# A bias-table tile 32 bytes longer: every later SBUF tile moves from 32 past a multiple of 64 bytes to a multiple of 64

## Chip, cores and metric

The kernel runs on one core of a Trainium2 chip. The metric is the device time of one execution in microseconds. Three runs of the kernel before took 2123.62, 2129.89 and 2130.25 us, median 2129.89 us.

## What is computed

A decoder trunk of two layers over 256 tokens of 2048 channels, batch 1, all in float32:

```python
cond = silu(c)
for i in range(2):
    sh1, sc1, g1, sh2, sc2, g2 = split(cond @ w_ada[i] + b_ada[i], 6)
    h = rmsnorm(x, norm_g[i, 0]) * (1 + sc1) + sh1
    y = pool_mixer(h) if i == 0 else moba_attention(h, w_qkv, w_o, rel_table)
    x = x + g1 * y
    h = rmsnorm(x, norm_g[i, 1]) * (1 + sc2) + sh2
    u = causal_conv3(h @ w_up[i]) + conv_b[i]        # 2048 -> 2 * 5632
    x = x + g2 * ((silu(u_gate) * u_val) @ w_down[i])
return rmsnorm(x, final_g)
```

The pool mixer takes trailing-window means and one 512 x 512 product per group; the attention is one causal block of 256 tokens with a T5 relative-position bias, whose 32 x 16 table `rel_table` is the table of this change.

## The kernel before

Activations lie with channels on the 128 partitions and the 256 tokens along the row. Every large product (`w_up`, `w_down`, `w_qkv`, `w_o`) is made as three float32r matmuls in place of one float32 matmul: weights and activations are each split into a rounded part `hi` and a rest, and `hi*hi`, `hi*rest` and `rest*hi` are summed in PSUM (`group_T`, function `products`):

```python
pe.matmul(o, hi[:, kk, w], h[:, 0:S], ...)     # stationary 128 x 128, moving 128 x 256
pe.matmul(o, hi[:, kk, w], h[:, S:S2], ...)
pe.matmul(o, lo[:, kk, w], h[:, 0:S], ...)
```

So in nearly all products a 128 x 128 block of weights (`hi` or `lo`) is the stationary operand, loaded before its matmul, and 256 tokens of an activation tile are the moving operand. Which activation tile that is differs by product: the normed input `h` for `uv` and `ug` (value and gate half of `w_up`) and for `k` and `q`; the tile `act` for `d` (`w_down`); the tile `o` for `wo` (`w_o`). The value projection `v` is turned round (`v_group`): `h` is stationary, and 512 columns of `hi` or `lo` are moving.

Weights arrive in pieces of 1 MiB (`w_load`, queue of SP) in five buffers `raw`; for each half of a piece ScalarE writes `hi` by a copy, VectorE writes `lo` by a subtraction (`w_use`), and three halves later (LAG) TensorE makes the 24 matmuls of that half (`run_half`). Beside this stream run the sums of the conditioning on VectorE (`acc`, `accs`), and convolutions, gates, norms and attention as tasks between halves.

SBUF is laid out by pools. `const` (one buffer for each tile) comes first, then `wp` (`raw`, `hi`, `lo`), then `work` (`act`, `o`, `acc` and the rest). Within a pool a tile begins where the one before ends, rounded up to 32 bytes. The last two tiles of `const` are made in `bias_rows`:

```python
st = const.tile([P, BUCKETS + 1], F32, name="starts")    # 132 bytes a partition, takes 160
rel = const.tile([BUCKETS, H], F32, name="rel")          # 16 floats, 64 bytes
```

`starts` begins at a multiple of 64, so `rel` and all that follows begin 32 bytes past one. Places in bytes of a partition, from the built programs:

```
tile                           before    mod 64   after     mod 64
xT (const)                     18240     0        18240     0
h, pool_room (const)           36864     0        36864     0
starts (const)                 72448     0        72448     0
rel (const)                    72608     32       72608     32
raw, 5 buffers (wp)            72672..   32       72704..   0
hi, 5 buffers (wp)             113632..  32       113664..  0
lo, 5 buffers (wp)             134112..  32       134144..  0
act, o, x, home (work)         156640..  32       156672..  0
acc (work)                     189664    32       189696    0
```

Rows within `hi`, `lo`, `h`, `act` and `o` are cut at multiples of 512 bytes, so a matmul's operand begins at the same place mod 64 as its tile. Before, `h` is thus the one large operand of the products at a multiple of 64; `hi`, `lo`, `act` and `o` are not.

Every operation of PE, DVE and ACT is recorded by a helper and has line 50 in the profile (L50); groups are told apart by the names of their tiles.

Of the kernel before, what the change touches and what calls it, by code (L numbers as in the profile page):

```python
# [9 lines left out]
F32 = mybir.dt.float32  # L10
# [8 lines left out]
EPS = 1e-6  # L19
# [6 lines left out]
def bucket_starts():  # L26
    """First distance of each T5 bucket (the buckets are intervals of distances)."""
    exact = BUCKETS // 2

    def bucket(n):  # L30
        if n < exact:
            return n
        big = exact + int(math.log(n / exact) / math.log(MAX_DIST / exact) * (BUCKETS - exact) + 1e-9)
        return min(big, BUCKETS - 1)

    of = [bucket(n) for n in range(4 * MAX_DIST)]
    return [next((n for n, b in enumerate(of) if b >= want), 1 << 20) for want in range(BUCKETS)]


class InOrder:  # L40
    """An engine whose instructions keep the order they are written in, once `on` is set."""

# [14 lines left out]
def trunk(ctx: ExitStack, tc: tile.TileContext, x, c, norm_g, w_ada, b_ada, pool_w, pool_scale, w_qkv, w_o,  # L57
# [35 lines left out]

# [1 line left out]
    ident = const.tile([P, P], F32, name="ident")  # L95
# [13 lines left out]

# [1 line left out]
    def rows_of(ap1):  # L111
        return ap1.rearrange("(k p) -> k p", p=P)

    def load_rows(name, rows, parts, eng):
        """The tiles of up to 128 rows each; parts: (first row, count, source)."""
        tiles = []
        for done in range(0, rows, P):
            n = min(P, rows - done)
            r = wt([P, P], "vec", 4, f"{name}_r{done}")
            for lo, cnt, src in parts:  # L120
                a, b = max(lo, done), min(lo + cnt, done + n)
                if a < b:
                    eng.dma_start(r[a - done:b - done, :], src[a - lo:b - lo, :])
            tiles.append((done, n, r))
        return tiles
# [8 lines left out]

# [1 line left out]
    c_rows = load_rows("cT", KD, [(0, KD, rows_of(c[0]))], nc.sync)  # L136
# [16 lines left out]
    def transposed(j, name):  # L153
        """Two channel blocks of the input tiles."""
        ps = aux(name)
        for jj in range(2):
            for t in range(NT):
                pe.transpose(ps[:, jj * S + t * P:jj * S + (t + 1) * P],
                                    xn[t][:, (j + jj) * P:(j + jj + 1) * P], ident)
        return ps  # L160
# [15 lines left out]

# [1 line left out]
    mod = const.tile([P, L, 6, KD], F32, name="mod")  # L178
# [4 lines left out]
    def mod_done(l, ch, j0, n, sums):  # L183
        """Columns j0..j0+n of a chunk from their sums."""
        js = slice(j0, j0 + n)
# [23 lines left out]
    def ada_add(l, ch, k, r):  # L209
        """One contraction block on the vector engine: acc += cond[k] * rows."""  # L210
        if (l, ch) not in ada:
            ada[l, ch] = wt([P, D], "acc", 1, f"acc{l}_{ch}")
            ve.tensor_scalar(ada[l, ch], r, cond[:, k:k + 1], None, op0=ALU.mult)
        else:
            a = ada[l, ch]
            ve.scalar_tensor_tensor(a, r, cond[:, k:k + 1], a, op0=ALU.mult, op1=ALU.add)

    def ada_side(l, ch, k):
        """Beside the main stream; the sum over partitions by squares of 32, then over the four quadrants."""
        def use(r):  # L220
# [21 lines left out]
    def slice_load(ch, s, q, pair):  # L242
        """Part of the contraction for 512 columns of a chunk of layer 0, or of two chunks side by side."""
        nk, w = (2, 2) if pair else (4, 1)
# [10 lines left out]
    def slice_use(ch, s, q, pair):  # L255
        """Some blocks of the contraction by TensorE as a row, the others by VectorE."""
        on_pe = PE_BLOCKS[ch if ch < 3 else 3 if s == 0 else 4]
# [45 lines left out]

# [1 line left out]
    sq = {}  # L305
# [23 lines left out]
    def rstd_tokens(m):  # L329
        """1/sqrt(m + EPS) with tokens on partitions, [128, NT]; a Newton step on the table's root."""  # L330
        s = wt([P, NT], "st", 8, "st_s")
# [13 lines left out]
    def root_ready():  # L345
        """Brings the root's table in before the norm needs it."""
        d = wt([P, 1], "st", 8, "st_d")
        ac.activation(d, mean_c, AF.Sqrt)
# [9 lines left out]
    def split(dst, j0, n, src):  # L358
        """An exact sum of two float32r parts: dst[.., :S] the rounded value, dst[.., S:] the rest."""
        hi = dst[:, j0:j0 + n, 0:S]  # L360
        ac.activation(hi, src, AF.Copy)
        ve.tensor_tensor(dst[:, j0:j0 + n, S:S2], src, hi.bitcast(F32), op=ALU.subtract)
# [6 lines left out]
    def scaled(dst, src, l, i, j, vec):  # L369
        """src * g * (1 + scale) + shift of one channel block."""  # L370
        a, b = gsc[:, l, i, j:j + 1], mod[:, l, 3 * i, j:j + 1]
# [5 lines left out]
    def h_block(l, i, j):  # L377
        """One channel block of x * rstd * g * (1 + scale) + shift, in two parts."""
        sh = mod[:, l, 3 * i, j:j + 1]
# [24 lines left out]

# [1 line left out]
    steps = []  # L406
# [20 lines left out]
    def run_tasks(n=1, upto=-1):  # L427
        """The next n tasks, and all up to the last that reads the banks of a group up to `upto`."""
        while tasks and (n > 0 or any(g <= upto for g, _ in tasks)):
            tasks.pop(0)[1]()  # L430
            n -= 1
# [6 lines left out]
    def group_T(src, nk, c0, rhs, done, name, home=None, each=None):  # L438
        """512 columns of src against the transposed activations; done(part) with part(f) the four sums.

        With a home in SBUF the sum is built there, a piece of the stream at a time.
        """
        box = {}
# [58 lines left out]

# [1 line left out]
    acts = {}  # L504
# [6 lines left out]
    def conv_task(o, part, group, f, l, j, then=None):  # L511
        """The causal depthwise convolution and its bias of one channel block."""
        def go():
# [10 lines left out]
    def residual(part, f, g, j):  # L524
        """x += gate * sum."""
        ve.scalar_tensor_tensor(xT[:, j, :], part(f), g[:, j:j + 1], xT[:, j, :], op0=ALU.mult, op1=ALU.add)

    def updated(part, g, og, f):
        """The last of a residual's sums, of two blocks: x and its squares."""
        j = og * 4 + f  # L530
# [131 lines left out]

# [1 line left out]
    bias_dram = dram.tile([H, S + P], F32, name="bias_dram")  # L664

    def bias_rows():
        """e[h, 127 + n] = rel_table[bucket(n), h], and NEG for negative n: rows of every Toeplitz bias."""
        starts = bucket_starts() + [1 << 20]
        st = const.tile([P, BUCKETS + 1], F32, name="starts")
        for b, v in enumerate(starts):  # L670
            nc.gpsimd.memset(st[:, b:b + 1], float(v))
        rel = const.tile([BUCKETS, H], F32, name="rel")
        nc.gpsimd.dma_start(rel, rel_table)
# [20 lines left out]
    def bias_tile(hg):  # L694
        """[p, h, m] = e[h, p + m]; a query p of block t meets key s at m = 255 - s + 128 * (t - 1)."""
        b = wt([P, 4, S], "t4", T4, f"bias{hg}")
# [43 lines left out]
    def scores(hg, t):  # L740
# [7 lines left out]
        for h0 in range(0, 4, per):  # L748
# [4 lines left out]
            bb = b[:, h0:h0 + per, 0:S]  # L753
            # key s reads m = 255 - s for the last block of queries, 127 - s for the first
            br = bb[:, :, n - 1::-1]
# [19 lines left out]
    def heads_out(hg, h0):  # L775
        """Two heads: transposed probabilities times values, split for the output projection."""
        v = att["v", hg]
# [48 lines left out]

# [1 line left out]
    PAD = 16  # L828
# [29 lines left out]
    def pool_sums(g):  # L858
        """Sums over the trailing window, by doubling."""
        w, cur = WINDOWS[g], pool["h"]  # L860
# [12 lines left out]
    def pool_less(g):  # L873
        """The window's mean minus the token."""
        d = pool_d(g)
# [5 lines left out]
    def pool_product(g, f):  # L881
        """One block of columns of the group's matrix."""
        d, w = pool_d(g), pool["w"][g]
# [5 lines left out]
    def pool_out(g):  # L889
        """x += gate * layer_scale * y."""  # L890
        for f in range(GB):
# [3 lines left out]

# [1 line left out]
    fin = {}  # L897

    def final_scaled(og, f, n):
        """x * final_g of n channel blocks."""  # L900
        if f == 0:
# [10 lines left out]
    def final_block(og):  # L912
        """Four channel blocks, tokens back on partitions."""
        if og == 0:
# [30 lines left out]

# [1 line left out]
    ends = []  # L947
# [184 lines left out]
```

## Time and profile before

| | us |
|---|---|
| runs | 2123.62, 2129.89, 2130.25 (median 2129.89) |
| profiled execution, span of its instructions | 2127.2 |
| PE busy in it | 2075.7 (98%) |
| DVE busy | 1643.2 (77%) |
| ACT busy | 958.5 (45%) |
| PE's share of the chain that ended last | 95% |

The profile gives the span of the execution it shows; a device time of its own is not listed beside the three runs, among which the span lies. Matmuls overlap in the records (each is shown for some 280 ns, and the next begins some 120 ns later), so what a matmul costs is read from the distance between starts: the length of an unbroken stretch of one product in the chain of waits, divided by its matmuls.

### The profile page before, as it was taken

How to read it: one execution, taken by the hardware profiler on the slowest of the kernel's cores; microseconds unless marked ns; L12 is line 12 of the kernel's file. 1: busy time of each engine (PE TensorE's matmuls, PEld its weight loads, DVE VectorE, ACT ScalarE, POOL GpSimd, SP SyncE). 2: the span in 40 equal slices, each digit the busy share in tenths (PEclk: the TensorE clock that was granted, in tenths of full speed). 3: DMA queues.
4: the chain of work that ended last, by engine and by line, in shares of the span. 5: the costliest groups of instructions: out<-in, count | busy, mean ns of one | idle time of the engine just before them, and what ended most of it. 6: DMA issues, size and time to landing. Idle time of an engine off the chain costs nothing.

```text
span 2127.2 us, 38504 instructions
## 1 busy us (share of the span) xinstructions
PE 2075.7 (98%) x16292; PEld 1971.2 (93%) x16292; DVE 1643.2 (77%) x2023; ACT 958.5 (45%) x1206; POOL 12.0 (1%) x64
## 2 busy tenths in 40 slices
PE   6888999999999999999999999999999999999998
PEld 2435999999999999999999999999999999999998
DVE  6877899799779898997787878779775666556665
ACT  3112633566444335444544444445443454434443
POOL 1000000000000000000000000000000000000000
PEclk8988999999999999999999999999999999999999
DMA  9998999555998989896888888578765555555551
GB/s 351 352 349 323 345 327 334 199 181 197 335 333 289 353 311 313 302 326 210 310 296 310 297 309 297 179 272 286 273 220 186 190 179 196 181 180 192 184 181 57
DMA packets 236445, 558.78 MB, mean 263 GB/s; under 512 B 9272, under 2 KB 9592, under 8 KB 221680
## 3 DMA queue, kind: packets, MB, share of 16 engines
q1 hardware_dynamic: 234800, 553.17, 74.5%
q8 instruction: 127, 2.08, 0.4%
q0 software_dynamic: 896, 2.49, 0.3%
q10 hardware_dynamic: 576, 0.67, 0.1%
q14 instruction: 46, 0.38, 0.0%
HBM read 554.17 MB, written 2.12 MB: 262 GB/s over the span
## 4 chain that ended last, share of the span: by engine, by line
PE 95%; DVE 2%; DMA 1%; ACT 1%; issue 1%; ACTq 0%; SPq 0%; DVEq 0%
PE d L50 24%; PE uv L50 23%; PE ug L50 23%; PE wo L50 4%; PE k L50 4%; PE q L50 4%; PE v L50 4%; PE row L50 2%; PE pp L50 2%; PE mods L50 1%; DMA ws<-in_w_ada_dram 1%; DVE accs L50 1%; DVE pool_room L50 1%; PE po L50 0%; PE sc L50 0%
## 5 line engine op out<-in xcount | busy, mean ns | idle before, releaser
L50 DVE TENSOR_TENSOR lo<-w,hi 128x1024 fp32r<-128x1024 f32 x656 | 793.6, 1221 | 318.2 <-ACT hi L50 317.4
L50 ACT ACTIVATE hi<-w 128x1024 fp32r<-128x1024 f32 x656 | 682.0, 1057 | 674.9 <-PE d L50 226.7
L50 PE MATMUL d<-act,hi 128*128 128x256 f32 x2816 | 506.7, 283 | 0.0
L50 PE MATMUL uv<-h,hi 128*128 128x256 f32 x2816 | 500.9, 280 | 3.9 <-ACT h L50 3.9
L50 PE MATMUL ug<-h,hi 128*128 128x256 f32 x2816 | 498.6, 280 | 0.0
L50 PEld LDWEIGHTS d<-act,hi 128*128 128x128 f32 x2816 | 438.1, 192 | 0.0
L50 PEld LDWEIGHTS uv<-h,hi 128*128 128x128 f32 x2816 | 433.0, 189 | 4.6 <-ACT h L50 4.2
L50 PEld LDWEIGHTS ug<-h,hi 128*128 128x128 f32 x2816 | 431.3, 188 | 0.0
L50 PE MATMUL d<-act,lo 128*128 128x256 f32 x1408 | 396.1, 283 | 0.0
L50 PE MATMUL uv<-h,lo 128*128 128x256 f32 x1408 | 395.1, 281 | 0.0
L50 PE MATMUL ug<-h,lo 128*128 128x256 f32 x1408 | 394.1, 280 | 0.0
L50 PEld LDWEIGHTS d<-act,lo 128*128 128x128 f32 x1408 | 269.2, 192 | 0.0
L50 PEld LDWEIGHTS uv<-h,lo 128*128 128x128 f32 x1408 | 265.6, 189 | 0.0
L50 PEld LDWEIGHTS ug<-h,lo 128*128 128x128 f32 x1408 | 264.6, 188 | 0.0
L50 DVE SCALAR_TENSOR_TENSOR acc<-wa,cond,acc 128x2048 f32<-128x2048 f32 x105 | 246.3, 2346 | 9.6 <-DMA wa<-in_w_ada_dram 9.4
L50 DVE SCALAR_TENSOR_TENSOR accs<-ws,cond,accs 128x512 f32<-128x512 f32 (+1 forms) x179 | 157.4, 882 | 20.4 <-DMA ws<-in_w_ada_dram 9.4
L50 PE MATMUL k<-h,hi 128*128 128x256 f32 x512 | 93.3, 284 | 1.1 <-ACT h L50 1.1
L50 PE MATMUL wo<-o,hi 128*128 128x256 f32 x512 | 92.8, 284 | 0.0
L50 PE MATMUL q<-h,hi 128*128 128x256 f32 x512 | 90.8, 280 | 0.0
L50 PE MATMUL row<-ws,cond 128*1 128x512 f32 x152 | 82.3, 669 | 8.2 <-DMA ws<-in_w_ada_dram 8.2
L50 PEld LDWEIGHTS k<-h,hi 128*128 128x128 f32 x512 | 79.7, 190 | 2.3 <-ACT h L50 1.4
L50 PE MATMUL v<-hi,h 128*128 128x512 f32 x256 | 80.5, 396 | 0.0
(157 smaller groups left out, 1762.2 us busy)
## 6 DMA issues: line engine op xcount, KB each, us to landing
w<-in_w_up_dram SPq DMA_DIRECT2D x176, 1024.0 KB, 5.2
wa<-in_w_ada_dram SPq DMA_DIRECT2D x112, 1024.0 KB, 6.3
w<-in_w_down_dram SPq DMA_DIRECT2D x88, 1024.0 KB, 5.1
ws<-in_w_ada_dram SPq DMA_DIRECT2D x56, 1024.0 KB, 8.1
w<-in_w_qkv_dram SPq DMA_DIRECT2D x48, 1024.0 KB, 6.3
ws<-in_w_ada_dram SPq DMA_DIRECT2D x48, 512.0 KB, 6.5
w<-in_w_o_dram SPq DMA_DIRECT2D x16, 1024.0 KB, 5.3
pw<-in_pool_w_dram SPq DMA_DIRECT2D x4, 1024.0 KB, 9.1
```

The source lines that it names most:

```text
L50: ins = call(*args, **kwargs)
```

## The change

`rel` gets 24 columns in place of 16 and is used through its first 16; it takes 96 bytes in place of 64, and everything placed after it lies 32 bytes higher, as the table above shows. No instruction is added, removed or moved: the instructions stand in the same order on all five engines, with the same shapes. (The rest of the diff strips comments and docstrings.)

```diff
     def bias_rows():
...
         for b, v in enumerate(starts):
             nc.gpsimd.memset(st[:, b:b + 1], float(v))
-        rel = const.tile([BUCKETS, H], F32, name="rel")
+        rel = const.tile([BUCKETS, H + 8], F32, name="rel")[:, :H]
         nc.gpsimd.dma_start(rel, rel_table)
```

## Rows read from the trace of the kernel before

**Rows 1.** The page, busy time of each engine over the span.

```profile
PE 2075.7 (98%) x16292; PEld 1971.2 (93%) x16292; DVE 1643.2 (77%) x2023; ACT 958.5 (45%) x1206; POOL 12.0 (1%) x64
```

**Rows 2.** The page, the chain that ended last, by engine and by line.

```profile
PE 95%; DVE 2%; DMA 1%; ACT 1%; issue 1%; ACTq 0%; SPq 0%; DVEq 0%
PE d L50 24%; PE uv L50 23%; PE ug L50 23%; PE wo L50 4%; PE k L50 4%; PE q L50 4%; PE v L50 4%; PE row L50 2%; PE pp L50 2%; PE mods L50 1%; DMA ws<-in_w_ada_dram 1%; DVE accs L50 1%; DVE pool_room L50 1%; PE po L50 0%; PE sc L50 0%
```

**Rows 3.** Waits of PE over the span: us in total, times, longest.

```profile
PE mods L50 <- DVE accs L50: 10.7, 4, 4.3
...
PE uv L50 <- ACT h L50: 3.9, 2, 2.7
```

**Rows 4.** Windows: stretch, length, busy us (instructions) by engine, PEclk, DMA, GB/s.

```profile
core 0: us, PE busy (x) PEld busy (x) DVE busy (x) ACT busy (x) POOL busy (x), PEclk, DMA share, GB/s
0.00:200.00 200.00, 164.77 (x593) 81.07 (x594) 146.76 (x256) 46.43 (x69) 8.96 (x60) 0.87 0.95 341
200.00:260.00 60.00, 57.26 (x473) 57.16 (x473) 51.11 (x57) 35.51 (x50) 0.00 (x0) 0.94 0.98 360
640.00:760.00 120.00, 120.00 (x1007) 120.00 (x1007) 112.46 (x133) 49.79 (x52) 0.00 (x0) 1.00 0.90 329
1640.00:2045.00 405.00, 405.00 (x3426) 405.00 (x3426) 239.21 (x277) 188.51 (x209) 0.00 (x0) 1.00 0.57 186
```

**Rows 5.** Chain in order of time, products with `h` moving: start, us, matmuls.

```profile
216.63 5.60 PE uv L50 x48
1452.95 22.40 PE uv L50 x192
1725.37 22.61 PE uv L50 x192
2021.05 22.61 PE ug L50 x192
973.10 5.60 PE q L50 x48
```

**Rows 6.** Chain in order of time, products with `act` or `o` moving.

```profile
525.81 92.14 PE d L50 x768
1277.54 69.11 PE wo L50 x576
1815.83 92.16 PE d L50 x768
```

**Rows 7.** Chain in order of time: `v` (512 columns moving), `sc` (plain float32, 256).

```profile
1174.05 11.19 PE v L50 x48
1046.79 1.73 PE sc L50 x8
```

**Rows 8.** The page, counts: line, engine, op, shapes, xcount, busy us, mean ns.

```profile
L50 PE MATMUL d<-act,hi 128*128 128x256 f32 x2816 | 506.7, 283 | 0.0
L50 PE MATMUL uv<-h,hi 128*128 128x256 f32 x2816 | 500.9, 280 | 3.9 <-ACT h L50 3.9
L50 PE MATMUL ug<-h,hi 128*128 128x256 f32 x2816 | 498.6, 280 | 0.0
L50 PE MATMUL d<-act,lo 128*128 128x256 f32 x1408 | 396.1, 283 | 0.0
L50 PE MATMUL k<-h,hi 128*128 128x256 f32 x512 | 93.3, 284 | 1.1 <-ACT h L50 1.1
L50 PE MATMUL wo<-o,hi 128*128 128x256 f32 x512 | 92.8, 284 | 0.0
L50 PE MATMUL v<-hi,h 128*128 128x512 f32 x256 | 80.5, 396 | 0.0
```

**Rows 9.** Groups of VectorE by form, the same operation on operands at different places.

```profile
L50 DVE TENSOR_TENSOR lo<-w,hi 128x1024 fp32r<-128x1024 f32 x656 | 793.6, 1221 | 318.2 <-ACT hi L50 317.4
L50 DVE TENSOR_TENSOR pool_room<-pool_room 128x1024 f32<-128x1024 f32 x4 | 4.9, 1214 | 0.0
```

## Prediction

> **What bounds the kernel now.** The busy shares come first: PE is busy for 98% of the span, DVE for 77% [rows 1]. Overlapping matmuls make a busy share flattering, so the chain of waits is read next: 95% of the time to the last instruction runs through PE, nearly all of it in the big products `d`, `uv`, `ug`, `wo`, `k`, `q`, `v` [rows 2]. The waits of PE confirm it: the longest sum is 10.7 us, from the conditioning at the start, and the stream itself loses some 4 us to a wait [rows 3]. Windows then split the span: up to 200 us the DMA engines are 95% busy at 341 GB/s and bound the work; from then on PE has work without a break, at a granted clock of 1.00, which is the 2.4 GHz level [rows 4]. So after 200 us the time is a number of matmuls times the distance between their starts, and a nanosecond more or less in that distance counts in full.
>
> That distance is read from unbroken stretches of the chain. With `h` moving, 48 matmuls take 5.60 us and 192 take 22.40 us: 116.7 ns. In other stretches 192 take 22.61 us: 117.8 ns [rows 5]. I count about as much of the stream at one level as at the other and use 117.3 for `uv` and `ug`, 116.7 for `k` and `q`. With `act` or `o` moving, 768 take 92.14 or 92.16 us and 576 take 69.11: 120.0 ns each time [rows 6]. The shapes, the weights and the clock are the same. What differs is the moving tile: `h` begins at a multiple of 64 bytes, `act` and `o` 32 past one. The weights `hi` and `lo` lie 32 past in both. `v` has it the other way round: stationary `h` on the multiple, moving weights 32 past, 512 columns, 11.19/48 = 233.1 ns [rows 7].
>
> **The change part by part.** No instruction is added, taken away or moved, and no wait changes; 32 bytes of address are all there is.
>
> *The moving operand.* `act` and `o` come to lie as `h` does. `d` has 2816 + 1408 matmuls, `wo` 512 and half as many with `lo` [rows 8]: 4224 + 768 = 4992, each from 120.0 to `h`'s 117.3: 2.7 ns x 4992 = 13.5 us. For `v`, whose 256 and 128 matmuls [rows 8] are one start each, I take the same 2.7 ns: 384 x 2.7 = 1.0 us.
>
> *The stationary operand.* No row has a 256-column float32r matmul with both operands on the multiple, so its distance b is bounded. From above by `h` moving, 117.3: the weights' place plays no part. From below by `v`: take 233.1 as two lots of 256 columns at b plus the 2.7 ns for a misplaced moving row; then b = (233.1 - 2.7)/2 = 115.2, lower only if there is something that the rows do not show, and higher by half of whatever a matmul costs once, which `v` pays once per 512 columns. I take b = 116, nearer the lower end, since the split of `v` rests on a row with its stationary operand on the multiple. That gives, below 117.3, another 1.3 ns on `uv` and `ug` (2 x 4224 = 8448 matmuls [rows 8]): 11.0 us; 0.7 ns on `k` and `q` (2 x 768 = 1536): 1.1 us; and 1.3 ns on `d` and `wo` (4992): 6.5 us.
>
> A rule speaks against this second term. The Trainium skill, TensorE: Matmul & The Clock Gate, section "Step-by-step: what each phase is for", says that PE reads weights and moving data through two ports of their own, so that a load takes no bandwidth from the running matmul. By that rule the second term is nothing and the sum ends at the first. No row shows a load's place changed alone, so it is rival 1.
>
> *VectorE and ScalarE.* They read and write the same tiles. A 1024-element operation takes 1221 ns on operands 32 past and 1214 ns on operands at the multiple [rows 9]: 7 ns x 656 = 4.6 us of VectorE's time at most. I count nothing, because that time lies beside PE; if VectorE were the bound it would be worth those 4.6 us.
>
> *DMA.* No transfer of the trace lands at a multiple of 64 in bulk, so the first 200 us are bounded only from the side: they run at 341 GB/s, and the fastest window at 360 [rows 4], so at most 200 x (1 - 341/360) = 11 us could be won. A loss of the same size cannot be excluded by a row. I take 0: the rate is within 5% of the fastest that the trace shows.
>
> *Is the gain covered by something else?* The tightest window is 640 to 760: VectorE 112.5 of 120 us, DMA 329 GB/s [rows 4]. A stream faster by 2% asks 336 GB/s and 96% of VectorE. Both still fit; a gain beyond 6% would make VectorE the bound there. Later windows have room: 239 of 405 us of VectorE.
>
> Sum: 13.5 + 1.0 + 11.0 + 1.1 + 6.5 = 33.1 us off the span of 2127.2. The median of the runs stands 2.7 us above that span, and I carry the difference over: 2129.9 - 33.1 = 2096.8, say **2097 us**. With b at its ends (115.2 and 117.3) the forecast runs from 2085 to 2115.
>
> **Rivals.**
>
> 1. *Only the moving row counts.* `h` products stay at 116.7 to 117.8, `d` and `wo` join them: 14.5 us, 2115 us. For it: the distance differs between `d` and `uv` with weights in the same place. Against it: `v` leaves room for less than `h`'s distance.
>
> 2. *Time goes by the 64-byte pieces an operand touches.* A moving row of 1024 bytes at 32 past touches 17 pieces, on the multiple 16; `d` would go from 120.0 to 120.0 x 16/17 = 112.9. `h` moving already touches 16 and yet needs 117.3, so what holds it there must be the weights (9 pieces, then 8), and it would fall too. Price: 8448 x 4.4 + 1536 x 3.8 + 4992 x 7.1 + 384 x 7.1 = 37.2 + 5.8 + 35.4 + 2.7 = 81 us, 2049 us. For it: TensorE can stream faster than this, since `sc`, with two clocks a column, needs 1.73/8 = 216 ns for 256 columns [rows 7], or 108 for one. Against it: 233.1 for 33 pieces fits, but twice `h`'s 116.7 fits as well.
>
> 3. *Equal places collide (slower).* `d` and `wo` are the products in which moving and stationary operand lie equally (both 32 past), and they are the slow ones; `uv` and `v` have them 32 apart, and `v` needs twice 116.6, as `uv` does. If two reads at equal places meet in one part of the memory, the change makes all products equal and all slow: 120.0 for 256 columns, 240 for 512. Price: 8448 x 2.7 + 1536 x 3.3 + 384 x 6.9 = 22.8 + 5.1 + 2.6 = 30.5 us, 2160 us. It decides if `ug` rises towards 120. Against it: the load asks for data at half the moving stream's pace or less, so that an offset of 32 bytes cannot keep the two apart for a whole matmul.
>
> 4. *The place is not the cause.* `act` and `o` differ from `h` also in where in SBUF they lie at large and in who wrote them last. Then nothing changes, 2130 us. For it: `h` itself has two levels, 116.7 and 117.8, at the same address [rows 5], so something else moves the distance by 1 ns. Against it: `d` and `wo` sit at 120.0 in every stretch, whichever of four buffers they read. By the Trainium skill, SBUF — State Buffer, section "Specifications (TRN2)", the memory's lines are 16 bytes; 32 is a multiple of that, so by this rule both places would serve alike and this rival would hold. The rows at 117 and 120 speak against the rule, but do not show the cause.
>
> **How the numbers follow.** About 0.3% (6.4 us) is what a measurement of this kernel can tell from no change. Forecast 0.38, rival 1 0.27, rival 2 0.15, rival 3 0.08, rival 4 0.12. Forecast and rivals 1 and 2 are faster by over 0.3%: 0.80. Rival 4 is the same: 0.12. Rival 3 is slower: 0.08. Forecast and rivals 1 and 4 hold only 0.77, so the range has to take in rival 2: from 2045, a little under its 2049, to 2132, a little over no change. That leaves out rival 3.
>
> **What the profile after would show.** First term right: the stretches of `d` take 89 to 90 us for 768 matmuls, not 92.1, and `wo` 67 for 576. Second term right: 192 of `ug` or `uv` take 22.3 us, below the 22.40 that they reach now; at 22.4 to 22.6 it is rival 1, at 21.7 rival 2, at 23.0 rival 3. `v`: 48 in 11.1 us or less. VectorE's `lo` stays near 1221 ns, and the window up to 200 us stays at 341 GB/s. The forecast is wrong if `d` stays at 120.0, if `ug` rises, or if PE begins to wait in the stream for `lo` or for a landing, which would mean that the gain was made and given back.

## The result and the profile after

The changed kernel took 2152.61 us (median of four runs, 2151.99 to 2153.99), the kernel before 2129.86 beside it: ratio 1.0108 [1.0091, 1.0126]. It is slower by 1.1%, some 23 us, and lies outside the predicted range, on the other side of no change.

The page of the changed kernel, busy times, chain by engine and by line, and the subtraction of VectorE:

```profile
PE 2099.1 (98%) x16292; PEld 1998.1 (93%) x16292; DVE 1644.3 (76%) x2023; ACT 959.6 (45%) x1206; POOL 12.0 (1%) x64
...
PE 95%; DVE 2%; DMA 1%; ACT 1%; issue 1%; ACTq 0%; SPq 0%; DVEq 0%
PE uv L50 24%; PE ug L50 24%; PE d L50 24%; PE k L50 4%; PE q L50 4%; PE wo L50 4%; PE v L50 4%; PE row L50 2%; PE pp L50 2%; PE mods L50 1%; DMA ws<-in_w_ada_dram 1%; DVE accs L50 1%; DVE pool_room L50 1%; PE po L50 0%; PE sc L50 0%
...
L50 DVE TENSOR_TENSOR lo<-w,hi 128x1024 fp32r<-128x1024 f32 x656 | 794.9, 1222 | 346.2 <-ACT hi L50 345.8
```

Beside [rows 1, 2, 9]: PE's busy time grew by 23.4 us with the same 16292 matmuls, PE has the same 95% of the chain, and `uv` and `ug` gained a point each; `lo` takes 1222 ns, as before. The waits of PE and the windows of the changed kernel, as in [rows 3] and [rows 4]:

```profile
PE mods L50 <- DVE accs L50: 11.2, 4, 4.8
...
PE uv L50 <- ACT h L50: 3.9, 2, 2.7
```

```profile
0.00:200.00 200.00, 161.76 (x594) 79.03 (x594) 148.46 (x259) 47.09 (x70) 8.96 (x60) 0.89 0.93 347
200.00:260.00 60.00, 58.96 (x474) 58.94 (x475) 49.83 (x54) 35.57 (x49) 0.00 (x0) 0.95 0.94 342
640.00:760.00 120.00, 120.00 (x1002) 120.00 (x1002) 110.37 (x125) 48.62 (x51) 0.00 (x0) 1.00 0.89 325
1640.00:2045.00 405.00, 405.00 (x3378) 405.00 (x3377) 235.97 (x273) 182.65 (x202) 0.00 (x0) 1.00 0.55 183
```

No wait is new, the transfers of the first 200 us run at 347 GB/s against 341, and the granted clock of the two late windows is 1.00 as before. But from 1640 to 2045 PE, busy without a gap, gets through 3378 matmuls where it got through 3426. The time has gone into the distance between matmuls and nowhere else. The chain of the changed kernel in order of time (start, us, what) says which:

```profile
215.02 5.76 PE uv L50 x48
...
531.39 92.16 PE d L50 x768
...
646.60 23.04 PE ug L50 x192
...
1186.71 10.89 PE v L50 x48
...
1290.51 69.11 PE wo L50 x576
...
1838.03 92.16 PE d L50 x768
...
2045.39 23.04 PE ug L50 x192
```

- `uv`, `ug`: 23.04/192 = 120.0 ns in every stretch, where [rows 5] had 116.7 or 117.8. The two levels are gone.
- `d`, `wo`: 92.16/768 and 69.11/576 = 120.0 ns, exactly as in [rows 6]. The move to a multiple of 64 gave them nothing.
- `v`: 10.89/48 = 226.9 ns, 6 ns *less* than in [rows 7]. Its matmuls of 512 columns go the other way than all the rest.

Averages over all unbroken starts of the two traces give the sum: `uv` and `ug` 8448 x (120.0 - 117.27) = 23.1 us; `k` and `q` 1536 x 3.1 = 4.8 us; `v` 384 x -5.9 = -2.3 us. That is +25.6; the stream's first matmul stood 2.0 us earlier (201.0 against 203.0 us); together +23.6, and the profiled span grew from 2127.2 to 2151.8, by 24.6.

### The profile page after: what moved, and what is told of

The parts are those of the page before. It is cut to its first block, busy times and chain, and to the rows that moved or that the text cites. A ratio compares the mean times of both kernels' runs of the same rounds, so it can differ in the third digit from the quotient of the medians.

```text
span 2151.8 us, 38504 instructions
## 1 busy us (share of the span) xinstructions
PE 2099.1 (98%) x16292; PEld 1998.1 (93%) x16292; DVE 1644.3 (76%) x2023; ACT 959.6 (45%) x1206; POOL 12.0 (1%) x64
## 4 chain that ended last, share of the span: by engine, by line
PE 95%; DVE 2%; DMA 1%; ACT 1%; issue 1%; ACTq 0%; SPq 0%; DVEq 0%
PE uv L50 24%; PE ug L50 24%; PE d L50 24%; PE k L50 4%; PE q L50 4%; PE wo L50 4%; PE v L50 4%; PE row L50 2%; PE pp L50 2%; PE mods L50 1%; DMA ws<-in_w_ada_dram 1%; DVE accs L50 1%; DVE pool_room L50 1%; PE po L50 0%; PE sc L50 0%
## 5 line engine op out<-in xcount | busy, mean ns | idle before, releaser
L50 DVE TENSOR_TENSOR lo<-w,hi 128x1024 fp32r<-128x1024 f32 x656 | 794.9, 1222 | 346.2 <-ACT hi L50 345.8
L50 PE MATMUL uv<-h,hi 128*128 128x256 f32 x2816 | 513.4, 285 | 3.9 <-ACT h L50 3.9
L50 PE MATMUL ug<-h,hi 128*128 128x256 f32 x2816 | 510.1, 283 | 0.0
L50 PEld LDWEIGHTS uv<-h,hi 128*128 128x128 f32 x2816 | 442.9, 193 | 4.5 <-ACT h L50 4.1
L50 PEld LDWEIGHTS ug<-h,hi 128*128 128x128 f32 x2816 | 440.2, 192 | 0.0
L50 PE MATMUL uv<-h,lo 128*128 128x256 f32 x1408 | 399.9, 284 | 0.0
L50 PEld LDWEIGHTS uv<-h,lo 128*128 128x128 f32 x1408 | 272.1, 193 | 0.0
L50 PEld LDWEIGHTS ug<-h,lo 128*128 128x128 f32 x1408 | 270.5, 192 | 0.0
L50 PEld LDWEIGHTS wo<-o,hi 128*128 128x128 f32 x512 | 79.8, 192 | 0.1
```

Source lines behind the costliest of these rows:

```text
L50: ins = call(*args, **kwargs)
```

## The experiments

The theory after the result: what counts is not an operand's place by itself but the **distance** between two places, that of the weights which PE loads for the next matmul and that of the row which it is streaming. Equal places are slow where 256 columns move. Before, `d` and `wo` had weights and moving tile equal (both 32 past), `uv` did not; the change made all equal. (`hi` and `lo` always have the same place, so the weights of a matmul and those loaded for the next one lie alike; that the load for the next one is what counts is assumed.) The rival: each operand's place counts for itself, or the large-scale addresses do.

The table below repeats the results; distances are means of unbroken starts over the whole trace, in ns, `v` for 512 columns. Ratios are to the kernel before, run beside each.

```
kernel            us        ratio [95%]               uv, ug   d       wo      k, q    v
before            2129.86   -                         117.3    120.0   119.9   116.8   233.3
after             2152.61   1.0108 [1.0091, 1.0126]   120.0    120.0   119.9   119.9   227.4
e1_weights_back   2108.62   0.9908 [0.9893, 0.9923]   116.8    116.7   116.7   116.7   233.3
e2_h_shifted      2130.19   1.0008 [0.9995, 1.0021]   117.3    120.0   119.9   116.9   233.3
e8_all_32         2155.77   1.0129 [1.0102, 1.0156]   120.0    120.0   119.9   119.9   227.4
e5_weights_64     2075.21   0.9746 [0.9733, 0.9759]   114.9    114.3   116.9   115.3   229.4
e6_v_halves       2154.93   1.0127 [1.0104, 1.0150]   120.0    120.0   120.0   120.0   2 x 120.0
e7_nudged         2069.41   0.9718 [0.9690, 0.9747]   113.9    114.1   114.0   114.5   229.1
```

**The weights put back.** From the kernel before, a gap of 32 bytes behind the weights moves only `act`, `o` and what follows; `hi` and `lo` stay 32 past a multiple of 64:

```diff
+    wp.tile([P, 8], F32, tag="gap", name="gap", bufs=1)
     while pending:
```

> The kernel before with 32 bytes left free between the weights' parts and the work pool: h at 0, hi and lo at 32, act and o at 0 past a multiple of 64; raw stays at 32. Theory A (a load and a moving row at equal places mod 64 slow each other, whatever the place): no product has equal places any more, so d and wo go from 120.0 to 116.7-117.8 ns and uv, ug, k, q stay there; v stays at 233; 13 to 16 us under before, 2114 to 2117 us. Theory B (the weights do best at 32, the moving row at 0, each for itself): the same, 2114 to 2117. Theory C (what slowed the changed kernel is another tile that moved, in the work pool): d stays at 120.0, and uv and ug are at 120.0 too, about 2152 us.

2108.62 us, faster than the kernel before by 0.9%, and 5 us below the 2114 to 2117 that were expected. Its chain in order of time:

```profile
525.13 89.60 PE d L50 x768
...
816.78 22.40 PE ug L50 x192
...
1166.09 11.19 PE v L50 x48
...
1269.21 67.20 PE wo L50 x576
```

`d` and `wo` fell from 120.0 to 116.7 ns (89.60/768, 67.20/576): 4992 x 3.3 = 16.5 us, and the mean of `uv` and `ug`, 116.8 for 117.3, gives 8448 x 0.47 = 4.0: together 20.5, and 20.0 us were gained. `act` and `o` lie on the multiple here as in the changed kernel, where the same products stand at 120.0. So the place of the moving tile alone does not set the distance. Against the changed kernel the weights have moved, and `raw` with them; which of the two counts, the scan below tells, where `hi` and `lo` alone move.

**The activation moved.** From the kernel before, a gap in `const` ahead of `h` moves everything from `h` on: `h` comes to lie 32 past, and weights, `act` and `o` on the multiple:

```diff
         pool["inv"] = inv
+        const.tile([P, 8], F32, name="gap")
```

> The change's places for weights and work pool (all at 0), reached by 32 free bytes ahead of h, so that h lies at 32. Theory A (equal places): uv, ug, k, q have places 32 apart again and return to 116.7-117.8 ns; d and wo (0 and 0) stay at 120.0; v (h at 32, weights at 0) goes back from 226.7 to 233; 2124 to 2132 us. Theory B (each place for itself): h moving at 32 and weights at 0 are both bad, so uv and ug stay at 120.0 or get slower, 2150 us or more.

2130.19 us, ratio 1.0008. The chain:

```profile
527.13 92.14 PE d L50 x768
...
824.53 22.40 PE ug L50 x192
...
1175.55 11.19 PE v L50 x48
...
1279.07 69.11 PE wo L50 x576
...
1772.07 22.61 PE uv L50 x192
```

Every place mod 64 is the opposite of the kernel before, and every distance is the same: 92.14 for `d`, 69.11 for `wo`, 22.40 and 22.61 for the two levels of `uv` and `ug`, 11.19 for `v`. The weights on the multiple and `h` off it serve as well as the reverse. What both kernels share is the differences.

**All of it 32 past.** The changed kernel with the same gap: `h`, weights, `act` and `o` all 32 past a multiple of 64, so all differences as in the changed kernel:

> The change with 32 free bytes ahead of h: h, weights' parts, act and o all lie 32 past a multiple of 64, none at a multiple. Theory A (only the distance between the two places counts): as in the changed kernel, 120.0 ns in uv, ug, k, q, d, wo, 226.7 in v, 2149 to 2156 us. Theory B (each place for itself): h moving at 32 adds to it, uv and ug above 120.0, and v is no longer at 226.7.

2155.77 us, against 2152.61 for the changed kernel (their intervals overlap), and the same distances to 0.05 ns. The chain:

```profile
648.93 23.04 PE ug L50 x192
...
1114.55 10.89 PE v L50 x48
...
1840.25 92.16 PE d L50 x768
```

Being at a multiple of 64 is worth nothing that these runs show. This settles the main question, as far as moves of 32 bytes go: the distance decides, the place does not.

**Which distances.** The changed kernel with the tiles `hi` and `lo` made 64 columns longer and used from a place that changes every four pieces of the stream, through a list, with four buffers `raw` in place of five to have the room:

```diff
+PLACES = (0, 1, 2, 4, 6, 8, 10, 12, 14, 16, 24, 32, 64)
...
+        o = PLACES[i // 4 % len(PLACES)]
-                hi = wp.tile([P, 2 * C], F32R, tag="hi", name=f"hi{i}_{half}", bufs=HB)
+                hi = wp.tile([P, 2 * C + 64], F32R, tag="hi", name=f"hi{i}_{half}", bufs=HB)[:, o:o + 2 * C]
```

(`lo` likewise. The places are counted in columns of four bytes; a second kernel has 16, 15, 17, 18, 20, 28, 36, 40, 44, 48, 52, 56 and 60.)

> The changed kernel with hi and lo cut from tiles 64 floats longer, at 0, 4, 8, 16, 24, 32, 40, 48, 56, 64, 96, 128 or 256 bytes from the tile's start, four pieces of the stream each in turn (and four raw buffers in place of five, to make room: more waits, the total is not compared). h, act and o lie at a multiple of 64. Read: the distance of matmuls by place. Theory A with two halves of a 64-byte line: 120.0 at 0, 64, 128 and 256, 116.7-117.8 at 32 and 96, and something between at the others. If the line is longer than 64 bytes, 64 or 128 differ from 0. If 4 or 8 bytes are enough to part the two reads, 4 and 8 are already at 117. v moves the weights, so for v the same scan tells the place of the moving row: 226.7 at 0 and 64, 233 at 32 by the rows so far.

> The same scan with other places of the weights: 60, 64, 68, 72, 80, 112, 144, 160, 176, 192, 208, 224 and 240 bytes past the multiple of 256 at which h, act and o lie (four raw buffers again, the total is not compared). Theory A mod 256: 224 gives 116.7 as in the version with the weights back at 32 past 64 (they lay at 224), 64 gives 113.8 again, and 192 (64 on the other side) shows whether the sign matters. If only the place mod 64 counts, 64 and 192 are at 120.0. A place shorter than 113.8, towards the 108 that plain float32 streaming shows for one clock a column, would be the best version.

They ran 2133.3 and 2130.64 us once each, which a mixture of places says little by. What they were made for is the distance between starts by the place of the loaded weights past the moving row, in bytes mod 256; it is worked out from the starts of some 950 to 1350 matmuls with 256 columns for each place (64 stands in both kernels, 113.8 in the first and 113.7 in the second):

```
bytes  0      4      8      16     24     32     40     48     56     60
ns     120.0  118.3  115.6  118.4  118.8  118.3  119.1  120.2  117.8  119.5
bytes  64     68     72     80     96     112    128    144    160    176
ns     113.8  118.3  118.3  118.8  119.3  119.9  118.7  119.1  119.9  118.1
bytes  192    208    224    240    256
ns     116.2  116.7  116.7  119.4  120.0
```

Three things are seen. The distance 256 repeats 0, and buffers and rows that differ by other multiples of 256 stand alike, while 64 and 128 differ from 0, and 96 from 224: as far as tried, the relation repeats every 256 bytes, not every 64 or 128, and the halves of a 64-byte line that were expected at first do not fit. The sign counts: at 48 no stretch is below 117.8, at 208, which is 48 the other way, all stand at 116.7. And there is no smooth course: 8 and 64 are good, 112 nearly as bad as 0.

A mean can hide two levels. Half by half, 192 stands at 113.3 in some stretches (`ug`) and at 117.8 in others (`d`, `wo`), the same two levels as 64 has, so the two means, 116.2 and 113.8, differ by the share of each level and do not part 64 from 192. At 48 the levels are 117.8 to 118.3 and, in `wo` and some of `d`, 123.6, which is slower than equal places.

For `v`, whose moving rows are the weights and whose load is `h`, the same traces give another order: 227.0 ns at equal places, 229.0 with the weights 112 past `h`, 229.7 at 64, 233.3 at 8, 233.4 at 32 and 192, 236.5 at 240, 237.4 at 68. With 512 columns moving, equal places are the quickest of the twelve that came up. That equal places as such make a load slow the stream is therefore not shown; what is shown is that the distance sets the time.

**The best distance for the whole stream.** The changed kernel with the weights at 64 past a multiple of 256, and `h`, `act`, `o` on one:

```diff
-        rel = const.tile([BUCKETS, H + 8], F32, name="rel")[:, :H]
+        rel = const.tile([BUCKETS, H + 24], F32, name="rel")[:, :H]
...
+    wp.tile([P, 48], F32, tag="gap", name="gap", bufs=1)
     while pending:
```

> The first scan had its shortest distance, 113.8 ns, with the weights 64 bytes past h or act, counted from multiples of 256 (120.0 at 0 and at 256). Here all weights' parts lie 64 past a multiple of 256 and h, act and o at a multiple of 256. Theory A, in the form that equal places are meant mod 256: uv, ug, d, k, q and wo at 113.8 ns; against the version with the weights back at 32 that is 14976 x 2.9 = 43 us, and v some 4 ns x 384 = 1.5 us: 2063 to 2068 us. Theory D (PE gains, but VectorE, ScalarE or the DMAs become late and give part of it back): 113.8 in the chain's stretches, yet new waits of PE for lo or hi, 2070 to 2095 us. Theory B (places mod 64 alone): all at 0 mod 64, so 120.0 everywhere, 2152 us.

2075.21 us, ratio 0.9746: faster than both kernels, by 54 and 77 us, through nothing but a longer table tile and a gap. It still missed what was expected, 2063 to 2068, by 7 us or more. The chain shows why:

```profile
522.19 90.45 PE d L50 x768
612.64 22.61 PE uv L50 x192
...
657.87 8.48 PE d L50 x72
666.52 78.96 PE d L50 x696
745.48 21.76 PE uv L50 x192
...
1256.13 67.84 PE wo L50 x576
...
1776.14 87.04 PE d L50 x768
1863.18 21.76 PE uv L50 x192
```

Two levels exist here too, and they are further apart: 21.76/192 = 113.3 and 22.61/192 = 117.8 ns, at the same addresses. From 203 us to the break in `d` at 666 the stream stands at 117.8 (90.45 for 768), then at 113.3 (78.96 for 696); `wo` falls back to 117.8, the second layer is at 113.3. PE's waits did not grow, and the tightest window of this kernel is

```profile
640.00:760.00 120.00, 120.00 (x1052) 120.00 (x1051) 115.63 (x137) 50.07 (x51) 0.00 (x0) 1.00 0.90 332
```

1052 matmuls for 1007 before [rows 4], VectorE at 115.6 of 120 us and DMA at 332 GB/s: the cover that the prediction worried about still held at 4% more matmuls.

**The load beside half a matmul.** In the changed kernel each 512-column matmul of `v` is made as two of 256, so that the load of `h` has 256 columns of stream beside it in place of 512:

```diff
-                        pe.matmul(ps, a, lo[:, kk, :], start=(k + kk == 0), stop=False)
-                        pe.matmul(ps, a, hi[:, kk, :], start=False, stop=False)
-                        pe.matmul(ps, r, hi[:, kk, :], start=False, stop=(k + kk == KD - 1))
+                        for n, (x, y) in enumerate(((a, lo), (a, hi), (r, hi))):
+                            for c0 in (0, S):
+                                pe.matmul(ps[:, c0:c0 + S], x, y[:, kk, c0:c0 + S], start=(k + kk + n + c0 == 0),
+                                          stop=(n == 2 and k + kk == KD - 1), skip_group_check=True)
```

> The changed kernel with each of v's matmuls over 512 columns made as two over 256 columns, so that the stationary block of h is loaded twice as often and a load runs beside all of the moving rows, not beside the first half. Theory A (a load beside a moving row at an equal place is what slows it): 120.0 ns for each, so 240 for 512 columns where the change has 226.7, 384 x 13 = 5 us more, 2155 to 2160 us. If instead the turned roles (h stationary) were what spared v, the halves take 113 to 114 each and the time stays at 2150 to 2154.

2154.93 us. The chain of this kernel, `q` and the doubled matmuls of `v`:

```profile
1069.57 5.76 PE q L50 x48
...
1096.73 5.76 PE v L50 x48
...
1110.87 11.51 PE v L50 x96
```

Two halves take 2 x 120.0 = 240 ns, where one matmul of 512 takes 226.9 in the changed kernel, 13 less. The whole time alone would not show it: it is 2.3 us over the changed kernel's, where 5 were expected, and the intervals of the two ratios overlap. So the turned roles are not what spared `v`; two matmuls of 256 columns, each with its load, cost more than one of 512. 226.9 is 120.0 + 106.9, and 256 columns at one a clock of 2.4 GHz would be 106.7 ns, an estimate: `v` can be read as one lot of 256 columns slowed by a load and one without. No run shows that split, and away from equal places it does not come out: before, `h` lay 32 past the moving weights, 233.3 less 106.7 leaves 126.6 for the slowed lot, and 256 columns at 32 take 118.3.

**Setting the level.** The version with the weights at 64, and at eight places in the order of halves a 64-column matmul into a PSUM tile that nobody reads:

```diff
+        if half == 1 and i in (3, 12, 30, 56, 146, 159, 171, 183):
+            pe.matmul(aux(f"nudge{i}")[:, :64], same, ones[:, :64], start=True, stop=True)
```

> The version with the weights 64 past, and eight small matmuls of 64 columns into a spare PSUM tile put into the stream (after pieces 3, 12, 30, 56, 146, 159, 171 and 183). That version shows two levels, 113.3 and 117.8 ns, and goes from the upper to the lower one where a matmul of 64 columns (modc) stands in the stream. If the level is a matter of how load and moving row happen to stand to each other in time, the small matmuls set it anew: the stretches from 200 to 666 us go to 113.3, and with parts of the attention and wo that is some 20 us less, at 8 x 0.25 us for the small matmuls: 2054 to 2062 us. If the level comes from what else runs then (the conditioning, DMA), it stays, 2075 to 2078. If VectorE (93% busy from 260 to 380 us) becomes late, 2062 to 2075 with waits for lo.

2069.41 us, ratio 0.9718, short of the 2054 to 2062 that were expected if the level is set anew. The chain, `mods` being 16 small matmuls of the conditioning:

```profile
237.84 5.44 PE uv L50 x48
...
247.48 1.68 PE mods L50 x16
...
250.56 5.65 PE uv L50 x48
...
273.17 5.65 PE ug L50 x48
278.83 0.17 PE nudge L50 x2
278.99 5.52 PE uv L50 x48
284.51 5.44 PE ug L50 x48
...
308.31 1.68 PE mods L50 x16
...
313.63 5.65 PE uv L50 x48
...
383.26 0.17 PE nudge L50 x2
383.43 5.52 PE ug L50 x48
388.94 16.32 PE uv L50 x144
...
658.64 10.86 PE d L50 x95
...
669.52 1.07 ACT hi L50
...
741.09 22.61 PE uv L50 x192
...
1260.10 57.19 PE wo L50 x504
```

(The nudge shows as x2 in the chain.) 48 matmuls take 5.44 us (113.3 ns each), after `mods` 5.65 (117.8), shortly after the nudge 5.44 again, after the next `mods` 5.65, after the next nudge 16.32 for 144 (113.3). So the level holds over hundreds of equal matmuls, and a small matmul in between sets it anew. So does a wait: near 670 us PE waited 0.6 us for `hi`, the only wait of its kind, and the level went from the lower (10.86 us for 95 with the breaks at both ends) to 117.8 (22.61 for 192) with no small matmul between. `wo` went from 117.8 to 57.19/504 = 113.5. Summed over the unbroken starts of each product (under 140 ns, or 250 for `v`), the distances come to 1763.9 us against 1778.3 without nudges, 14.4 less; but the time gained only some 6 us over the version without, within the spread of its five runs (2061.88 to 2077.57). Part of what was expected was lost because each `mods`, and the wait, put the level up again. Of the 14 us, 4.8 went ahead of the stream, whose first matmul stood at 202.7 us in this profile and at 197.9 in that of the version without; the nudges and the wait took most of the rest. The time also lies in the range that was given for a late VectorE, but PE never waits for `lo`.

## Why the prediction was wrong

- **What bounds the kernel** stood: PE nearly without a break after 200 us (57.3 of 60 us busy up to 260, at a granted clock of 0.94, and 1.00 in the later windows [rows 4]), a nanosecond of distance counting in full. Terms worked out as matmuls times a change of distance agree with the measured times, in the result and in e1.
- **The reading that failed is "What differs is the moving tile: `h` begins at a multiple of 64 bytes, `act` and `o` 32 past one."** It was one of two differences in the same rows: `d` also had moving tile and weights at equal places, and `uv` did not. The table of places showed both. I took the first as cause and left the second to rival 3.
- ***The moving operand*, 13.5 us for `d` and `wo`:** measured 0. They had equal places before (224 past a multiple of 256, both) and after (0, both). The same 13.5 us (16.5 as measured) is there when only one of the two is moved, e1. For `v` 1.0 us was forecast and 2.3 came. That the sign was right is luck: the term supposed that a moving row gains by lying on a multiple of 64, and in e8 `v` has the same 227.4 ns with its rows 32 past one.
- ***The stationary operand*, 11.0 and 1.1 us for `uv`, `ug`, `k`, `q`, and 6.5 for `d` and `wo`:** measured +23.1, +4.8 and 0. The bound "from above by `h` moving" was no bound: it supposed that bringing the weights to a multiple of 64 can't hurt. The lower bound rested on splitting 233.1 of `v` into two equal lots of 256 columns; e6 shows that a matmul of 512 columns is not two of 256 (226.9 against 240 at the same places).
- **VectorE, DMA and cover at nothing:** right. `lo` 1222 ns, DMA 347 GB/s, no new wait.
- **Rival 3** gave the right figure for 256 columns, 120.0 to the tenth, but not for 512. Its cause, two reads that meet in one part of the memory, is not shown, and the scan speaks against its simple form: 256 columns at 48 reach 123.6, and 512 are quickest at equal places. It was given 0.08 because "the load asks for data at half the moving stream's pace or less, so that an offset of 32 bytes cannot keep the two apart". That was a mechanism thought out, set against two rows that fitted the rival without remainder (`d` and `wo` equal and slow, `uv` unequal and quicker); the rows should have had the weight. Its 2160 is 7 us over the measured 2152.6: it priced `v` at 240, and `v` came to 227.4, worth 384 x 12.6 = 4.8 us. The stream's earlier start makes up 2.0.
- **Rival 1** leaned on the Trainium skill, TensorE: Matmul & The Clock Gate, section "Step-by-step: what each phase is for", by which the load of weights takes no read bandwidth from the running matmul. The runs disagree: in the scan, where only `hi` and `lo` move, the distance runs from 113.3 to 123.6 ns by their place, at a granted clock of 1.00; and from the changed kernel to e1, where `raw` moves with them, `d` goes from 120.0 to 116.7.
- **Rival 2** (64-byte pieces) is out: e8 and the changed kernel touch different numbers of pieces at the same 120.0.
- **Rival 4** was right that an address as such does not matter (e8), and its note of two levels at one address pointed at the level that e5 ran into. The 16-byte lines of the Trainium skill, SBUF — State Buffer, section "Specifications (TRN2)", don't explain the scan: places 64 and 80 past are both whole lines away and stand at 113.8 and 118.8, and 4 and 8 bytes, within one line, at 118.3 and 115.6.

What stays open is why the distances rank as they do, why they rank otherwise for 512 columns, and what in the chip repeats every 256 bytes. Parts of the memory that serve one reader at a time would give a collision at equal places, but no run here shows such parts, and the quick places 8 and 64 were found by trying.

## What to carry to other kernels

Where matmuls follow each other without a break and each has its own load of weights, look at the places of the two operands *against each other*, mod 256 bytes, and try a few distances with gaps of some bytes between pools: here that was worth 2.5% with no instruction changed. Rounding every tile to the same alignment is a way to make all places equal, which was a slow case here for 256 moving columns (and the quickest for 512). And when two rows differ in time, list every way in which they differ before naming one as the cause; here one experiment that moved one side alone (e1 or e2) separated them.

## What the runs showed of the hardware that was not expected

- A float32r matmul of 256 columns, with a load of 128 x 128 weights beside it, takes 113.3 to 123.6 ns from start to start at one granted clock, 1.00, by the distance of the two operands mod 256 bytes and by a level. Equal places take 120.0.
- The distance has two levels at the same addresses, 116.7 and 117.8 at a difference of 224, 113.3 and 117.8 at 64 and at 192; equal places have one, 120.0. The level holds until small matmuls or a wait come between, and these set it anew, up or down: in e7 `mods` and a wait of 0.6 us put it up, and a single 64-column matmul brought it down.
- A matmul of 512 columns is not two of 256: 226.9 ns at equal places, 240 as two matmuls. Its time, too, goes by the distance, but in another order: equal places are the quickest (227.0), 68 the slowest of those that came up (237.4).
